# A hybrid state-space and attention layer on one core: the operand stacks of the next two heads begun at the first row block instead of the second, and the low parts of the first queries computed ahead of the other preparations

## The chip, the cores and the metric

The kernel runs on one core of a Trainium2 chip. The time is the device time of one execution in microseconds; the number that counts is the median over the runs. Engine names are those of the profile: PE (TensorE), DVE (VectorE), ACT (ScalarE), POOL (GpSimd) and SP (SyncE, which here only issues transfers). SPq, POOLq and so on are the engines' own queues of transfer issues.

## The reference, cut to what matters

One layer of an encoder runs over 512 prompt rows and 8 x 16 sample rows, 640 rows in all. Only branch B, the attention, is touched by the change: 8 heads of width 64, with a bias by relative position.

```python
z = rms_norm(x, p['g_mix']) @ p['w_in']
u, q, k, v, g_ssm, g_att = jnp.split(z, cuts, axis=-1)
# prompt, by chunks of 64 rows; a chunk reads itself and up to 8 chunks before it
sc = jnp.einsum('nihd,nkhd->nhik', qc, kb).astype(jnp.float32) * scale + bias
p = jax.nn.softmax(sc, axis=-1).astype(v.dtype)
return jnp.einsum('nhik,nkhd->nihd', p, vb)
# sample: 16 new rows of each of 8 streams read 512 cached rows and themselves
```

The other branch is a state-space scan (`s5`). Both branches are gated, added, projected, and followed by a convolutional feed-forward part.

## The kernel before

All products are made in float32r with operands cut into a high and a low part. A weight unit is 128x1024; for each of its eight blocks PE does three pairs of matmuls of 320 columns (`mm3`, line 115, outputs `pb`). This stream of projections runs without pause: after the state input come v, k, q and 16 units of gates. Each segment of six matmuls is one `tick`. Beside it a generator, `side_work`, is advanced by a fixed share of a step per tick: first the scan (`s5`), then the attention (`attention`). So everything of the attention stands between segments of the projections in PE's stream, and every engine executes its instructions strictly in the order in which the program wrote them (the schedule is manual).

The attention takes two heads at a time (`hp` = 0 to 3, heads 2hp and 2hp+1). Each pair has 32 steps of the generator: four row blocks `t` of 128 prompt rows (two prompts per block, one per head, three steps apart), and a sample group after blocks 1 and 3. The dictionary `plan` holds what is done at each step; things of the same step run in the order in which `at` wrote them.

- `prompt`: step +0 two matmuls of scores into the single bank `sS` (queries `qs`, then their low parts `ql`, both against `ks`), the bias and row maximum on DVE (line 733, reading the bias `pb`), the exponential on ACT (line 693); step +4 the normalisation (lines 739 and 740); step +8 the transposes into the single bank `sT` (line 746) and their evacuation `eT` by ACT (line 687) or DVE (line 689) in turn. `prompt_pv` multiplies with v.
- `sample`: the same for 64 sample rows (lines 794 to 833), with cached keys `kc` and values `vc`, two transfers each, three buffers each, loaded by `load_kv` one step after the previous group's scores.
- `stacks(hp)`: makes the operands `ks` and `qs` of a pair of heads in four steps: the high parts of k on ACT (line 663), the low parts of k on DVE (line 668), then two transfers on SP that put the low parts into the other half of the partitions of `ks` together with the high parts of q on ACT (line 663), then two transfers on SP that copy the halves of `qs` (line 672). Both tiles have two buffers.
- `q_low(hp)`: the low parts `ql` of the queries, two DVE instructions (line 703), one buffer.
- The preparations ahead of the first pair: POOL zeroes the idle halves of `ql` (line 698) and all of `QB` (line 848), SP loads two biases, keys and values, DVE copies the sample queries into `QB` (line 852, two copies for each pair of heads).

The names `pb` and `h` are used for more than one thing: `pb` is a bank of a projection on PE's lines and the bias in line 733; `h` is any 128x640 tile of the heap. `wr`, `wh`, `wl` are a weight unit, its high and its low part.

Of the kernel before, what the change touches and what calls it, by code (L numbers as in the profile page):

```python
# [43 lines left out]
def body(nc, tc, d, ctx):  # L44
# [12 lines left out]
    def nm(s):  # L57
        uid[0] += 1
        return f"{s}{uid[0]}"
# [585 lines left out]
    def half(h2):  # L645
        return slice(64 * h2, 64 * h2 + 64)
# [3 lines left out]
    def stacks(hp):  # L650

        if hp > 3:
            return []
        k, q = (qk[0].tile([128, 2, 512], F32R, tag=t, name=nm(t), bufs=2) for t in ("ks", "qs"))
        kl = ht(F32R, 512).rearrange("p (a b) -> p a b", a=1)
        st_[hp] = (k, q)

        def hi(dst, src):  # L660
            for h2 in range(2):
                s = half(h2)
                A.activation(dst[s, h2, :], src[s, 0:512], AF.Copy)

        def lo(dst, src, h):
            for h2 in range(2):
                s = half(h2)
                V.tensor_tensor(dst[s, 0, :], src[s, 0:512], h[s, h2, :].bitcast(F32), op=OP.subtract)

        def move(dst, src):  # L670
            for h2 in range(2):
                S.dma_start(dst[half(1 - h2), h2, :].bitcast(F32), src(h2).bitcast(F32))
        return [lambda: hi(k, kT[hp]), lambda: lo(kl, kT[hp], k),
                lambda: (move(k, lambda h2: kl[half(h2), 0, :]), hi(q, qT[hp])),
                lambda: move(q, lambda h2: q[half(h2), h2, :])]

    def attention():
# [22 lines left out]
        def q_low(hp):  # L700
            for h2 in range(2):
                s = half(h2)
                V.tensor_tensor(ql[s, h2, :], qT[hp][s, 0:512], st_[hp][1][s, h2, :].bitcast(F32), op=OP.subtract)
# [6 lines left out]
        def at(t, fn):  # L710
            plan.setdefault(t, []).append(fn)
# [3 lines left out]
        def load_pb(h):  # L715
            if h < 8:
                pbs[h] = ap_.tile([128, 512], F32, tag="pb", name=nm("pb"))
                S.dma_start(pbs[h], d["pbias"][h])

        def prompt(t0, h, t):  # L720
            hp, h2 = h // 2, h % 2
            w = 128 * (t + 1)
            m = {}

            def a():
                sc = smps("sS")
                k, q = st_[hp]
                n = max(w, 256)
                ts = slice(128 * t, 128 * t + 128)
                mm(sc[:, :n], q[:, h2, ts], k[:, h2, 0:n], True, False)  # L730
                mm(sc[:, :n], ql[:, h2, ts], k[:, h2, 0:n], False, True)
                sb, mx = tiles()
                V.tensor_tensor_reduce(sb[:, :w], sc[:, :w], pbs[h][:, 512 - w:512], 1.0, -3.0e38,
                                       op0=OP.add, op1=OP.max, accum_out=mx[:, 1:2])
                m["e"], m["mx"] = exps(sb, w, mx), mx

            def n():
                e, mx = m["e"], m["mx"]
                V.reciprocal(mx[:, 4:5], mx[:, 3:4])
                V.tensor_scalar(e[:, :w], e[:, :w], mx[:, 4:5], None, op0=OP.mult)  # L740

            def b():
                e = m["e"]
                pt = smps("sT")
                for k in range(t + 1):
                    PE.transpose(pt[:, k * 128:k * 128 + 128], e[:, k * 128:k * 128 + 128], ident)  # L746
                m["eT"] = ap_.tile([128, 512], F32, tag="eT", name=nm("eT"), bufs=3)
                evac(m["eT"][:, :w], pt[:, :w])

            at(t0, a)  # L750
            at(t0 + 4, n)
            at(t0 + 8, b)
            return m

        def prompt_pv(t0, hp, t, ms):

            def c():
                if t == 0:
                    po[0] = smps("sP")
                for k in range(t + 1):  # L760
                    for h2, m in enumerate(ms):
                        h = 2 * hp + h2
                        mm(po[0][half(h2), 128 * t:128 * t + 128], vt_[k][:, h * 64:h * 64 + 64],
                           m["eT"][:, k * 128:k * 128 + 128], k == 0, k == t)
                if t == 3:
                    evac(att[hp][:, 0:512], po[0])

            at(t0, c)

        def load_kv(hp, g4):  # L770
            if g4 == 0:
                sbs[hp] = ap_.tile([128, 576], F32, tag="sbias", name=nm("sbias"), bufs=1)
                S.dma_start(sbs[hp], d["sbias"][hp])
            kc, vc = [], []
            for i in range(2):
                k = ap_.tile([128, 2, 512], F32, tag="kc", name=nm("kc"), bufs=3)
                S.dma_start(k, d["kc"][hp, g4, :, 2 * i:2 * i + 2])
                kc.append(k)
            for i in range(2):
                v = ap_.tile([128, 2, 4, 128], F32, tag="vc", name=nm("vc"), bufs=3)  # L780
                S.dma_start(v, d["vc"][hp, g4, :, 2 * i:2 * i + 2])
                vc.append(v)
            kvs[hp, g4] = (kc, vc)

        def sample(t0, hp, g4):
# [55 lines left out]
            at(t0 + 12, c)  # L841
            at(t0 + 15, e_)

        load_pb(0)
        load_pb(1)
        load_kv(0, 0)
# [2 lines left out]
        for hp in range(4):  # L849
            for h2 in range(2):  # L850
                s = slice(64 * h2, 64 * h2 + 64)
                V.tensor_copy(QB[s, hp, :, h2, :], qT[hp][s, 512:640].rearrange("p (n i) -> p n i", n=8))
            if hp == 0:
                q_low(0)
            yield

        t0 = 0
        nxt = [None]
        for hp in range(4):
            for t in range(4):  # L860
                ms = []
                for h2 in range(2):
                    ms.append(prompt(t0, 2 * hp + h2, t))
                    if t == 3:
                        at(t0 + 1, lambda h=2 * hp + h2: load_pb(h + 2))
                    t0 += 3
                    if t == 1 and h2 == 1:
                        at(t0, lambda hp=hp: nxt.__setitem__(0, stacks(hp + 1)))
                        for j in range(4):
                            at(t0 + (1, 3, 5, 7)[j], lambda j=j: nxt[0] and nxt[0][j]())  # L870
                prompt_pv(t0 - 3 + 12, hp, t, ms)
                if t == 3 and hp < 3:
                    at(t0, lambda hp=hp: q_low(hp + 1))
                if t % 2:
                    i = 2 * hp + t // 2
                    sample(t0, hp, t // 2)
                    if i < 7:
                        at(t0 + 1, lambda i=i: load_kv((i + 1) // 2, (i + 1) % 2))
                    t0 += 4
# [29 lines left out]
    def side_work():  # L909
        qk[0] = qctx.enter_context(tc.tile_pool(name="qk", bufs=1))  # L910
        yield from s5()
        side[2] = 172 / (247 - clock[0])
        yield from attention()
        qctx.close()
# [223 lines left out]
    h2 = xctx2.enter_context(tc.tile_pool(name="heap2", bufs=1))  # L1138
# [599 lines left out]
```

## Time and profile before

| | |
|---|---|
| median of 3 runs | 943.2 us (942.18 to 1254.34) |
| the profiled execution | 940.75 us |
| its span | 938.9 us, so 1.85 us lie around the span |
| PE busy | 906.8 us (97% of the span) |
| DVE, ACT, POOL busy | 627.1, 441.5, 134.4 us |
| granted clock of PE, mean | 0.993 of full speed |
| stretch of the attention | about 182 to 323 us |

PE is the engine that sets the time, so what matters is where PE stands idle and where its clock falls. The profile puts each idle time down to what ended it.

### The profile page before, as it was taken

The numbers are of one execution on the slowest core, as the hardware profiler recorded it, in microseconds if no ns is written. First come the engines' busy times: TensorE is split into PE (matmuls) and PEld (weight loads), VectorE is DVE, ScalarE is ACT, GpSimd is POOL, SyncE is SP. The second block draws the span as 40 slices with busy tenths as digits, with TensorE's granted clock in tenths as the row PEclk, the third lists the DMA queues.
The fourth block names the chain that finished last, engine by engine and source line by source line (L and its number), as shares of the span: only waits on it lengthen the run. The fifth ranks groups of instructions, "written<-read, shape, count | busy, mean of one in ns | idle before, by whom it ended". The sixth has DMA issues, their size and how long they took to land.

```text
span 938.9 us, 16523 instructions
## 1 busy us (share of the span) xinstructions
PE 906.8 (97%) x6534; PEld 868.9 (93%) x6534; DVE 627.1 (67%) x1261; ACT 441.5 (47%) x689; POOL 134.4 (14%) x230
## 2 busy tenths in 40 slices
PE   8999999999899999999998999999999999999995
PEld 8978999987787899999998989999999999999994
DVE  6783996376675444586777887667666667667545
ACT  7244112353443464434676456554555545554531
POOL 0121402300000000000013122221122212222200
PEclk9999999999999999999999999999999999999998
DMA  6744428657566432243548689898788887888733
GB/s 227 206 134 127 132 71 92 214 192 256 170 183 235 111 104 68 69 127 132 140 105 190 147 164 226 181 201 188 180 197 191 192 201 179 186 200 194 180 60 112
DMA packets 62429, 151.76 MB, mean 162 GB/s; under 512 B 20945, under 2 KB 24209, under 8 KB 62353
## 3 DMA queue, kind: packets, MB, share of 16 engines
q1 hardware_dynamic: 45392, 95.90, 33.4%
q0 software_dynamic: 16096, 54.03, 30.4%
q8 instruction: 51, 0.84, 0.3%
q10 hardware_dynamic: 864, 0.78, 0.2%
q14 instruction: 26, 0.20, 0.1%
HBM read 114.56 MB, written 8.21 MB: 131 GB/s over the span
## 4 chain that ended last, share of the span: by engine, by line
PE 72%; DMA 9%; DVE 7%; ACT 5%; issue 4%; POOL 1%; SPq 1%; DVEq 0%; POOLq 0%; ACTq 0%
PE pb L115 40%; PE sS L115 9%; PE sT L115 7%; PE sX L115 7%; PE sP L115 5%; DMA wl<-in_w 3%; DMA o_s<-SV 2%; DMA qs<-qs 1%; DMA fl<-s 1%; DMA pb<-in_pbias 1%; PE sX L822 1%; DVE h L1536 1%; DMA wr<-in_w 1%; ACT wh L107 1%; PE sT L746 1%
## 5 line engine op out<-in xcount | busy, mean ns | idle before, releaser
L115 PE MATMUL pb<-h,wh 128*128 128x320 f32 (+2 forms) x2000 | 384.4, 313 | 4.7 <-DVE h L1517 1.2
L115 PEld LDWEIGHTS pb<-h,wh 128*128 128x128 f32 x2000 | 313.4, 189 | 10.5 <-issue 3.3
L115 PE MATMUL pb<-h,wl 128*128 128x320 f32 (+2 forms) x1000 | 230.3, 310 | 0.4 <-DVE wl L112 0.4
L115 PEld LDWEIGHTS pb<-h,wl 128*128 128x128 f32 x1000 | 167.9, 188 | 0.9 <-DVE wl L112 0.7
L1300 POOL DMA_DIRECT2D fl<-s x41 | 35.7, 871 | 440.7 <-PE pb L115 259.0
L107 ACT ACTIVATE wh<-wr 128x1024 fp32r<-128x1024 f32 x50 | 52.7, 1054 | 80.3 <-PE pb L115 59.9
L112 DVE TENSOR_TENSOR wl<-wr,wh 128x1024 fp32r<-128x1024 f32 x50 | 61.0, 1221 | 39.5 <-ACT wh L107 39.3
L115 PE MATMUL sS<-h,wh 128*128 128x320 f32 x336 | 74.7, 309 | 0.0
L115 PE MATMUL sX<-h,fh 128*128 128x320 f32 x320 | 71.6, 311 | 0.0
L1298 ACT ACTIVATE fl<-s 128x1024 fp32r<-128x1024 f32 x41 | 43.3, 1057 | 56.1 <-PE sT L115 48.7
L115 PEld LDWEIGHTS sS<-h,wh 128*128 128x128 f32 x336 | 56.2, 188 | 0.0
L115 PE MATMUL sS<-h,wl 128*128 128x320 f32 x168 | 52.2, 311 | 2.9 <-DMA wl<-in_w 2.9
L693 ACT ACTIVATE sb<-sb,mx 128x128 f32<-128x128 f32 (+4 forms) x40 | 24.2, 605 | 64.0 <-DVE mx L692 49.4
L115 PEld LDWEIGHTS sX<-h,fh 128*128 128x128 f32 x320 | 54.1, 190 | 0.0
L1300 POOL DMA_DIRECT2D wl<-in_w x43 | 38.1, 887 | 86.9 <-ACT wl L1298 79.6
L1371 ACT ACTIVATE tmp<-tmp 128x512 f32<-128x512 f32 x22 | 13.9, 633 | 76.0 <-DVE tmp L1368 76.0
L115 PE MATMUL sX<-h,fl 128*128 128x320 f32 x160 | 49.6, 310 | 0.0
L1298 ACT ACTIVATE wl<-wr 128x1024 fp32r<-128x1024 f32 (+1 forms) x43 | 43.5, 1011 | 7.1 <-PE sS L115 6.0
L115 PE MATMUL sT<-h,gh 128*128 128x320 f32 x176 | 40.1, 315 | 4.4 <-DVE u L1457 4.4
L1299 ACT ACTIVATE wh<-wr 128x1024 fp32r<-128x1024 f32 (+1 forms) x43 | 43.1, 1003 | 0.0
L1299 ACT ACTIVATE fh<-s 128x1024 fp32r<-128x1024 f32 x41 | 42.9, 1046 | 0.0
L1368 DVE SCALAR_TENSOR_TENSOR tmp<-tmp,vec 128x656 f32<-128x656 f32 x44 | 39.5, 897 | 0.7
(339 smaller groups left out, 1678.0 us busy)
## 6 DMA issues: line engine op xcount, KB each, us to landing
wr<-in_w SPq DMA_DIRECT2D x112, 512.0 KB, 4.6
fl<-s POOLq DMA_DIRECT2D x41, 512.0 KB, 5.8
wl<-in_w POOLq DMA_DIRECT2D x39, 512.0 KB, 8.3
kc<-in_kc SPq DMA_DIRECT2D x16, 512.0 KB, 6.6
vc<-in_vc SPq DMA_DIRECT2D x16, 512.0 KB, 5.7
x<-in_x SPq DMA_DIRECT2D x7, 320.0 KB, 5.9
pb<-in_pbias SPq DMA_DIRECT2D x8, 256.0 KB, 6.6
h<-in_x SPq DMA_DIRECT2D x6, 320.0 KB, 4.5
```

The lines of the kernel that those rows point to most:

```text
L107: A.activation(hi, raws[u], AF.Copy)
L112: V.tensor_tensor(lo, raws[u], hi.bitcast(F32), op=OP.subtract)
L115: PE.matmul(ps, lhs, rhs, start=start, stop=stop)
L693: A.activation(sb[:, :w], sb[:, :w], AF.Exp, bias=mx[:, 2:3], accum_out=mx[:, 3:4])
L746: PE.transpose(pt[:, k * 128:k * 128 + 128], e[:, k * 128:k * 128 + 128], ident)
L822: PE.matmul(sx[32 * n:32 * n + 32, 192:320], m["eT"][:, k * 128 + 32 * n:k * 128 + 32 * n + 32], vc[n // 2][:, n % 2, k, :], start=(k == 0 ...
L1298: A.activation(lo, src, AF.Copy, scale=-1.0)
L1299: A.activation(hi, src, AF.Copy)
L1300: G.dma_start(lo, src if again is None else again, accum_op=OP.add)
L1368: V.scalar_tensor_tensor(c_t, a_t[:, j:L + j], vcol(C_CW + 3 * f + j), c_t, op0=OP.mult, op1=OP.add)
L1371: A.activation(g_t[:, 0:512], c_t[:, 0:512], AF.Gelu_apprx_tanh)
L1536: V.scalar_tensor_tensor(o[:, 0:b - a], h_[i][:, a:b], vcol(C_GO + i), rs, op0=OP.mult, op1=OP.mult)
```

## The change

Three things are moved; no instruction is added or taken away. First, `q_low(0)` stands ahead of the first loads and of `QB`, not behind the first two copies into it. Second, the four steps of `stacks(hp + 1)` begin after the second prompt of row block 0, not of row block 1: they stand at steps +7, +10, +13 and +16 of a pair of heads where they stood at +13, +15, +17 and +19. Third, with that the first of them sit among the prompts of blocks 0 and 1.

```diff
+        q_low(0)
         load_pb(0)
         load_pb(1)
         load_kv(0, 0)
...
                 V.tensor_copy(QB[s, hp, :, h2, :], qT[hp][s, 512:640].rearrange("p (n i) -> p n i", n=8))
-            if hp == 0:
-                q_low(0)
             yield
...
                     t0 += 3
-                    if t == 1 and h2 == 1:
+                    if t == 0 and h2 == 1:
                         at(t0, lambda hp=hp: nxt.__setitem__(0, stacks(hp + 1)))
                         for j in range(4):
-                            at(t0 + (1, 3, 5, 7)[j], lambda j=j: nxt[0] and nxt[0][j]())
+                            at(t0 + (1, 4, 7, 10)[j], lambda j=j: nxt[0] and nxt[0][j]())
```

On DVE, at the start of the attention, this stands in the kernel before (`ql` is the low part of the queries, `QB` the sample queries, `sb` the scores of the first two prompts):

```order
L112 TENSOR_TENSOR wl_1972<-wr_1789,wh_1971 128x1024
L852 COPY QB<-h_1405 64x8x16 x2
L703 TENSOR_TENSOR ql<-h_1405,qs_1727 64x512 x2
L852 COPY QB<-h_1482 64x8x16 x2
L852 COPY QB<-h_1547 64x8x16 x2
L852 COPY QB<-h_1612 64x8x16 x2
L733 ISA sb_2100,mx_2101<-sS_2097,pb_2053 128x128
```

In the changed kernel, the same place on DVE:

```order
L703 TENSOR_TENSOR ql<-h_1405,qs_1727 64x512 x2
L853 COPY QB<-h_1405 64x8x16 x2
L853 COPY QB<-h_1482 64x8x16 x2
L853 COPY QB<-h_1547 64x8x16 x2
L853 COPY QB<-h_1612 64x8x16 x2
L733 ISA sb_2100,mx_2101<-sS_2097,pb_2055 128x128
```

The low parts moved past the first two copies; all eight copies still stand ahead of the first line 733.

On SP, in the second pair of heads (`hp` = 1), from the second sample group's loads to the next biases, before:

```order
L100 DMA wr_2470<-in_w 128x1024
L777 DMA kc_2615<-in_kc 128x1024
L777 DMA kc_2617<-in_kc 128x1024
L781 DMA vc_2619<-in_vc 128x1024
L781 DMA vc_2621<-in_vc 128x1024
L100 DMA wr_2656<-in_w 128x1024
L672 DMA ks_2589<-h_2591 64x512 x2
L672 DMA qs_2590<-qs_2590 64x512 x2
L718 DMA pb_2726<-in_pbias 128x512
L718 DMA pb_2778<-in_pbias 128x512
```

and in the changed kernel:

```order
L100 DMA wr_2470<-in_w 128x1024
L672 DMA ks_2518<-h_2520 64x512 x2
L777 DMA kc_2621<-in_kc 128x1024
L777 DMA kc_2623<-in_kc 128x1024
L781 DMA vc_2625<-in_vc 128x1024
L781 DMA vc_2627<-in_vc 128x1024
L672 DMA qs_2519<-qs_2519 64x512 x2
L100 DMA wr_2662<-in_w 128x1024
L718 DMA pb_2726<-in_pbias 128x512
L718 DMA pb_2778<-in_pbias 128x512
```

The transfers of `ks` moved ahead of the four loads of keys and values; those of `qs` moved ahead of one weight load only and still stand behind the last `vc`. The other two pairs show the same.

On DVE, in the same pair of heads, around the first sample group (lines 799 and 801 are its bias and maximum; `sX` is its second bank), before:

```order
L740 TENSOR_SCALAR sb_2521<-sb_2521,mx_2522 128x256
L689 COPY h_1405<-sX_2397 64x64
L799 ISA sb_2599,mx_2600<-sS_2592,sbias_2411 128x512
L799 ISA mx_2600 128x1
L801 ISA sb_2599,mx_2600<-sX_2593,sbias_2411,mx_2600 128x64
L801 ISA mx_2600 128x1
L692 TENSOR_SCALAR mx_2600<-mx_2600 128x1
L739 RECIPROCAL mx_2570<-mx_2570 128x1
L740 TENSOR_SCALAR sb_2569<-sb_2569,mx_2570 128x256
L689 COPY eT_2626<-sT_2623 128x256
L668 TENSOR_TENSOR h_2591<-h_1266,ks_2589 64x512 x2
L733 ISA sb_2642,mx_2643<-sS_2639,pb_2325 128x384
```

and in the changed kernel:

```order
L668 TENSOR_TENSOR h_2520<-h_1266,ks_2518 64x512 x2
L739 RECIPROCAL mx_2525<-mx_2525 128x1
L740 TENSOR_SCALAR sb_2524<-sb_2524,mx_2525 128x256
L689 COPY h_1405<-sX_2397 64x64
L799 ISA sb_2603,mx_2604<-sS_2596,sbias_2411 128x512
L799 ISA mx_2604 128x1
L801 ISA sb_2603,mx_2604<-sX_2597,sbias_2411,mx_2604 128x64
L801 ISA mx_2604 128x1
L692 TENSOR_SCALAR mx_2604<-mx_2604 128x1
L739 RECIPROCAL mx_2575<-mx_2575 128x1
L740 TENSOR_SCALAR sb_2574<-sb_2574,mx_2575 128x256
L689 COPY eT_2632<-sT_2629 128x256
```

The low parts of k (line 668) moved from just ahead of a prompt of block 2 to just ahead of the normalisation that stands before the sample group.

## Rows read from the trace of the kernel before

**Rows 1.** Waits of PE from 140 to 325 us: total, times, longest.

```profile
PE sS L115 <- DMA qs<-qs: 3.3, 3, 1.6
PE sT L810 <- ACT eT L687: 2.2, 2, 1.4
```

**Rows 2.** PE in order of time, first prompts: start, length, instruction, idle before.

```profile
186.94 0.36 PE L115 MATMUL sS<-ks,ql 128*128 128x256 f32 x1 [0.99 <-issue]
...
189.35 0.58 PE L115 MATMUL sS<-ks,qs 128*128 128x256 f32 x1 [1.18 <-DVE mx L733]
...
192.96 0.28 PE L115 MATMUL sS<-ks,qs 128*128 128x256 f32 x1
```

**Rows 3.** DVE in order of time, the same place.

```profile
185.68 0.46 DVE L852 COPY QB<-h 64x128 f32<-64x128 f32 x2 [8.62 <-POOL QB L848]
186.15 1.40 DVE L703 TENSOR_TENSOR ql<-h,qs 64x512 fp32r<-64x512 f32 x2
187.57 1.40 DVE L852 COPY QB<-h 64x128 f32<-64x128 f32 x6
189.00 0.29 DVE L733 CUSTOM_DVE_ANT_0 sb<-sS,pb 128x128 f32<-128x128 f32 x1
```

**Rows 4.** POOL in order of time, the same place.

```profile
183.66 1.10 POOL L698 MEMSET ql<- 64x512 f32 x2
184.70 0.94 POOL L848 MEMSET QB<- 128x1024 f32 x1
```

**Rows 5.** SP in order of time, the first load into the attention's pool.

```profile
182.34 0.80 SPq L718 DMA_DIRECT2D pb<-in_pbias  x2
```

**Rows 6.** By stretch: length; busy PE, PEld, DVE, ACT, POOL; clock, DMA share, GB/s.

```profile
188.00:189.00 1.00, 0.17 (x2) 0.00 (x0) 0.92 (x6) 0.00 (x0) 0.00 (x0) 1.00 1.03 377
...
191.00:192.00 1.00, 1.00 (x5) 1.00 (x5) 0.21 (x1) 1.00 (x5) 0.00 (x0) 0.50 1.03 422
...
250.00:260.00 10.00, 9.05 (x103) 8.09 (x104) 5.43 (x20) 2.58 (x9) 0.00 (x0) 1.00 0.65 224
```

**Rows 7.** PE in order of time, the other waits.

```profile
235.56 0.65 PE L810 MATMUL sT<-ident,sb 128*128 128x128 f32 x4 [1.42 <-ACT eT L687]
...
250.95 0.36 PE L115 MATMUL sS<-ks,qs 128*128 128x256 f32 x1 [1.65 <-DMA qs<-qs]
...
252.58 0.31 PE L115 MATMUL sS<-ks,qs 128*128 128x256 f32 x1
...
283.28 0.35 PE L115 MATMUL sS<-ks,qs 128*128 128x256 f32 x1 [1.41 <-DMA qs<-qs]
...
287.23 0.66 PE L810 MATMUL sT<-ident,sb 128*128 128x128 f32 x4 [0.76 <-ACT eT L687]
```

**Rows 8.** SP in order of time, ahead of the third pair of heads.

```profile
228.90 12.66 SPq L781 DMA_DIRECT2D vc<-in_vc  x2
...
242.09 1.11 SPq L672 DMA_DIRECT2D ks<-h  x2
243.28 1.19 SPq L672 DMA_DIRECT2D qs<-qs  x2
244.57 1.12 SPq L718 DMA_DIRECT2D pb<-in_pbias  x2
```

**Rows 9.** The tile qs: issue to landing over its eight transfers.

```profile
DMA to landing us min/median/max: 4.4/6.7/7.7
```

**Rows 10.** The tile pb, as a bias: issue to landing over its eight transfers.

```profile
DMA to landing us min/median/max: 2.7/6.6/8.4
```

**Rows 11.** DVE in order of time, first line 733 of the third and fourth pair.

```profile
252.15 0.29 DVE L733 CUSTOM_DVE_ANT_0 sb<-sS,pb 128x128 f32<-128x128 f32 x1 [1.98 <-DMA pb<-in_pbias]
...
285.62 0.29 DVE L733 CUSTOM_DVE_ANT_0 sb<-sS,pb 128x128 f32<-128x128 f32 x1 [3.64 <-DMA pb<-in_pbias]
```

**Rows 12.** ACT in order of time, high parts of k in the second pair.

```profile
230.71 1.27 ACT L663 ACTIVATE ks<-h 64x512 fp32r<-64x512 f32 x2
```

**Rows 13.** DVE in order of time, low parts of k in the second pair.

```profile
231.36 1.40 DVE L668 TENSOR_TENSOR h<-h,ks 64x512 fp32r<-64x512 f32 x2 [0.66 <-ACT ks L663]
```

## The prediction

> **What bounds the kernel now.** The table of times gives PE 97% of the span, so the first view is that of PE's waits, cut to the stretch in which the attention runs beside the projections. It lists three waits for the transfer of `qs`, 3.3 us, and two for an evacuation `eT` by ACT, 2.2 us [rows 1]; two more, 0.99 us put down to "issue" and 1.18 us to DVE's row maximum, lie at the very first prompts [rows 2]. The reader is to see that these 7.7 us are all that an edit to the order of the attention can win in PE's idle time. PE in order of time then says where each wait lies. The two at the first prompts are 2.4 us apart. [...] Single waits of 1.42, 1.65, 1.41 and 0.76 us stand later [rows 7]; the rest of the 3.3 us, about 0.25, lies ahead of the second pair of heads.
>
> DVE and POOL tell what the first two waits hang on. DVE does nothing until POOL has zeroed `QB`, then copies, makes `ql`, copies again, and only then reaches the first line 733 at 189.00 [rows 3]; POOL ended at 185.64 [rows 4]. The "issue" wait is thus a wait for `ql`, whose part for the first head ended 0.7 us after 186.15, just before PE went on [rows 2, 3]. SP's order tells the `qs` waits: the transfers of `ks` and `qs` stand behind a load of `vc` that blocks SP for 12.66 us [rows 8], and `qs` lands 4.4 to 7.7 us after its issue [rows 9].
>
> **The change part by part.** *Low parts first.* The two instructions keep their 1.40 us [rows 3]. They need the memory of the scan's pool, as the first bias load does, and that load was issued at 182.34 [rows 5]; they wait for no POOL instruction, since POOL zeroes the other halves. So `ql` should be done near 183.8, well before PE asks at 186.94 - 0.99 = 185.95 [rows 2]: the wait of 0.99 goes. What is late next is line 733. Its eight `QB` copies still need POOL's end at 185.64 and 0.46 + 1.40 = 1.86 us [rows 3, 4], so it starts near 187.55, and PE's second prompt 0.35 us later as before (189.00 to 189.35), near 187.9. PE would be there at 189.35 - 1.18 - 0.99 = 187.18 [rows 2], so a wait of about 0.7 stays. Gain 189.35 - 187.9 = 1.45 us. Bounds: 0 if `ql` waits for something that holds DVE till 185.6, 2.17 if both waits go.
>
> *The clock.* From the second to the third prompt PE takes 192.96 - 189.35 = 3.6 us at half clock [rows 2, 6], so 1.8 us are lost. The single wait of 1.65 us that ends at 250.95 [rows 7] is followed by no such fall: the clock from 250 to 260 us is 1.00 [rows 6]. With one wait of 0.7 us left I take the whole 1.8; bounds 0 and 1.8. [...]
>
> *The stacks six to three steps earlier.* Per pair they are two instructions on ACT for k and two for q, 1.27 us each two [rows 12], two on DVE, 1.40 us [rows 13], and four transfers on SP. No work is added.
>
> On SP the transfers of `ks` pass four loads of keys and values; those of `qs` pass one weight load and remain behind `vc`. At the third pair `vc` frees SP at 241.56, so `qs` is issued from about 241.65 instead of 243.28, its second half 0.6 us later near 242.25, with no `ks` and no weight between it and `vc` [rows 8]. With the median 6.7 us it lands at 248.95, with the longest 7.7 at 249.95 [rows 9]; PE asks at 250.95 - 1.65 = 249.30 [rows 7]. I take the median, because two 128 KB transfers and a weight have left its way: all three `qs` waits go, 3.3 us [rows 1]. The lower bound leaves 0.6 at each of the two long ones, 2.1 us. What is late next is the bias `pb`: the first line 733 of the pair waited for it until 252.15, and in the fourth pair until 285.62 [rows 11]. Its issue moves up by the 1.11 us of `ks` [rows 8], to 243.4, and by its median of 6.6 us it lands at 250.0 [rows 10]. PE wants the bank of the scores back 252.58 - 250.95 = 1.63 us after the pair's first score [rows 7], that is at 250.93, so line 733 must start by 250.5: covered by half a microsecond, and open by 1.2 us with the longest 8.4.
>
> In the fourth pair the same chain (bias, line 733, exponential, `eT`, line 810) gave the wait of 0.76 [rows 7]. PE comes 1.41 us earlier, the chain at least 1.1 by the issue alone, and more by the shorter way: I take 0.76 as gained, bounds 0 and 0.76.
>
> On ACT and DVE the old place crowded the wait of 1.42 us at 235.56 [rows 7]: 1.40 us of low parts stood ahead of a line 733 [rows 13]. They now stand before the sample group's line 799, whose exponential the same evacuation also stands behind on ACT. So the chain is relieved at its end and loaded at its start: I take half of the 1.40, gain 0.7, bounds 0 and 1.42.
>
> Against it, in the first pair the high parts of k now enter ACT while it catches up: from 191 to 192 us it is busy throughout [rows 6]. Behind that, 1.27 us [rows 12] make the next `eT` late for PE; of this I take a third, 0.4 us, since two segments of projections stand between the two uses of its bank; bounds 0 and 1.27. In the third pair ACT was busy for 2.58 and DVE for 5.43 of the 10 us from 250 [rows 6], so there, and in the second, whose blocks are the same, I count nothing. SP now waits for the low parts of k ahead of four loads; who waits is the sample group of step +28, some 15 steps away.
>
> Sum: 1.45 + 1.8 + 3.3 + 0.76 + 0.7 - 0.4 = 7.6 us. Against the profiled execution: span 938.9 - 7.6 = 931.3, with 1.85 around it 933.15. That execution lies 2.45 us under the median of 943.2, so the median becomes **935.6 us**. Behind the attention the loads and splits of weights are started by PE's own progress, so I see nothing that gives the time back.
>
> **The rivals.** *The clock falls all the same.* For it: a wait of 0.7 us and a slow start of the softmax chain remain at the same place. Against: two waits, 2.17 us, came ahead of the fall [rows 2]. Gain 7.6 - 1.8 = 5.8, time 937.4.
>
> *One wait takes the place of the other.* The transfers are late not for their place in the queue but for the way itself: `qs` is still behind `vc`, and `pb` behind `qs`. If PE stands as long at the two long transitions and at line 810, the gain is 1.45 + 1.8 + 0.25 + 0.7 - 0.4 = 3.8, time 939.4. For it speaks that `pb` landed 1.2 us after `qs` [rows 7, 11]; against, that two of the four slow transfers between partitions leave that stretch.
>
> *Slower.* The moved stacks sit in the wrong place: 1.27 us on ACT and 1.40 on DVE [rows 12, 13] stand ahead of prompts of blocks 0 and 1, which have the shortest matmuls to hide behind. It decides when ACT and DVE together have less than 2.67 us to spare between the prompts of steps +6 and +12. Fully exposed in three pairs this costs 8.0 us, and as the chain is then late the two `eT` waits stay: 1.45 + 1.8 + 3.3 - 8.0 = -1.45, time 944.65. Against it: from 250 to 260 us ACT was idle for 7.4 and DVE for 4.6 us [rows 6].
>
> *It doesn't do what it says.* `ql` is held till POOL is done and SP's order hides the earlier transfers: 0 to 1 us, 942.7.
>
> **How the numbers follow.** Forecast 935.6 with 0.6, the clock 0.13, the replaced wait 0.15, slower 0.05, nothing 0.07. The forecast's own bounds: all upper ends, 2.17 + 1.8 + 3.3 + 0.76 + 1.42 = 9.45, give 933.75; the lower ends of single terms are the rivals. The range reaches from 932.5 (a microsecond under that for the spread of the runs, whose lower two differ by 1.0) to 941.5, which takes in the replaced wait with 2 us above it and leaves out the last two cases. A difference of 2%, 18.9 us, is about what a measurement of this kernel can tell from no change; all cases lie far inside: faster by more 0.01, within 0.98, slower by more 0.01.
>
> **What would show it.** In the changed kernel's trace: `ql` at 182 to 184 us on DVE, ahead of POOL's end; no wait of PE at its first `ql` matmul, one of 0.5 to 1 us at the second prompt; clock 1.00 from 189 to 193; no PE wait for `qs`; line 733 of a pair waiting less than 1 us for `pb`; 0.5 to 1 us left near line 810 of the second pair. The prediction is wrong if the clock still falls at the start, or if new waits of PE for `eT` or for line 799 come up between steps +8 and +20 of a pair.

## The result, and the profile after

| | before | after |
|---|---|---|
| median of 6 runs each | 942.31 us | 934.2 us (933.25 to 935.76) |
| ratio of the times, 95% interval | | 0.9932 (0.9915 to 0.9949) |
| profiled execution, its span | 940.75, 938.9 us | 934.26, 932.4 us |
| mean granted clock of PE | 0.993 | 0.995 |

One run of before, at 1254.34 us, is left out of the ratio. The changed kernel is faster: the interval of the ratio stands for a gain of 4.8 to 8.0 us on 942.31 us. The two medians are 8.1 us apart, a little more than that. The forecast was 935.6 us, with a gain of 7.6 us.

The waits of PE from 140 to 325 us, in the changed kernel (total, times, longest), answer to [rows 1]:

```profile
PE sS L115 <- DVE mx L733: 1.0, 1, 1.0
PE sX L115 <- ACT h L687: 0.9, 1, 0.9
PE sX L115 <- DVE h L689: 0.8, 1, 0.8
PE sT L810 <- ACT eT L687: 0.5, 1, 0.5
PE sT L746 <- ACT eT L687: 0.2, 1, 0.2
```

No wait for `qs` is left, and the one put down to "issue" at the start is gone. What stays is 3.4 us where 7.7 stood. But three lines are new: PE waits twice for the evacuation of the bank `sX`, 1.7 us together, where the prediction had nothing, and 0.2 us for an `eT` at line 746, in the first pair.

At the first prompts, PE, DVE and POOL of the changed kernel in order of time, against [rows 2 to 4]:

```profile
186.40 0.28 PE L115 MATMUL sS<-ks,qs 128*128 128x256 f32 x1
...
188.66 0.39 PE L115 MATMUL sS<-ks,qs 128*128 128x256 f32 x1 [0.99 <-DVE mx L733]
...
190.77 0.28 PE L115 MATMUL sS<-ks,qs 128*128 128x256 f32 x1
```

```profile
183.09 1.40 DVE L703 TENSOR_TENSOR ql<-h,qs 64x512 fp32r<-64x512 f32 x2 [4.71 <-DMA qs<-qs]
186.41 1.87 DVE L853 COPY QB<-h 64x128 f32<-64x128 f32 x8 [1.91 <-POOL QB L849]
188.31 0.29 DVE L733 CUSTOM_DVE_ANT_0 sb<-sS,pb 128x128 f32<-128x128 f32 x1
```

```profile
185.43 0.95 POOL L849 MEMSET QB<- 128x1024 f32 x1
```

`ql` is done before POOL is, and the eight copies run in one go of 1.87 us from POOL's end to the first line 733. The execution runs about 0.7 us later than the profiled one of before at this place (the last matmul of the scan ends at 183.00, in before at 182.28), so times are compared from that matmul's end below. The stretches answer to [rows 6]; the last figures but two are the granted clock:

```profile
188.00:189.00 1.00, 0.34 (x2) 0.34 (x3) 0.72 (x5) 0.14 (x1) 0.00 (x0) 1.00 0.90 322
191.00:192.00 1.00, 1.00 (x10) 1.00 (x8) 0.91 (x6) 1.00 (x3) 0.00 (x0) 1.00 0.98 332
250.00:260.00 10.00, 9.11 (x104) 7.08 (x103) 6.68 (x25) 3.45 (x9) 0.00 (x0) 1.00 0.57 190
```

From 191 to 192 us the clock is 1.00 and ten matmuls ran, where five ran at 0.50.

SP ahead of the third pair, against [rows 8]:

```profile
225.41 1.19 SPq L672 DMA_DIRECT2D ks<-h  x2
...
227.76 11.43 SPq L781 DMA_DIRECT2D vc<-in_vc  x2
239.28 1.10 SPq L672 DMA_DIRECT2D qs<-qs  x2
...
241.10 0.93 SPq L718 DMA_DIRECT2D pb<-in_pbias  x2
```

`qs` still stands behind the loads of `vc`, which hold SP for 11.43 us, but is the first thing behind them. The landing of the eight `qs` transfers and of the biases, from 170 to 330 us, against [rows 9, 10]:

```profile
DMA to landing us min/median/max: 4.6/5.3/6.8
```

```profile
DMA to landing us min/median/max: 2.7/5.9/8.0
```

And PE at three waits of the sample groups. The one of 1.42 us at line 810 in [rows 7] is now 0.47; the two of `sX` are new:

```profile
227.00 0.43 PE L115 MATMUL sX<-h,QB 128*128 128x64 f32 x2 [0.77 <-DVE h L689]
...
233.18 0.65 PE L810 MATMUL sT<-ident,sb 128*128 128x128 f32 x4 [0.47 <-ACT eT L687]
...
259.08 0.43 PE L115 MATMUL sX<-h,QB 128*128 128x64 f32 x2 [0.89 <-ACT h L687]
```

What the first of them waits for is seen on DVE, ahead of it, in order of time:

```profile
224.63 0.15 DVE L692 TENSOR_SCALAR mx<-mx 128x1 f32<-128x1 f32 x1
224.70 1.40 DVE L668 TENSOR_TENSOR h<-h,ks 64x512 fp32r<-64x512 f32 x2
226.13 0.16 DVE L739 RECIPROCAL mx<-mx 128x1 f32<-128x1 f32 x1
226.33 0.35 DVE L740 TENSOR_SCALAR sb<-sb,mx 128x256 f32<-128x256 f32 x1
226.71 0.23 DVE L689 COPY h<-sX 64x64 f32<-64x64 f32 x1
226.97 0.69 DVE L799 CUSTOM_DVE_ANT_0 sb<-sS,sbias 128x512 f32<-128x512 f32 x1
```

The low parts of k, 1.40 us, stand ahead of the copy out of `sX` that frees the bank for the sample group's second score product; between them are only the two short instructions of a normalisation. PE asks for the bank at 227.00 - 0.77 = 226.23 us, the copy ends at 226.94, and PE starts at 227.00.

The wait in the third pair is put down to ACT, but the chain is the same. The bank is emptied by two copies, one of them on ACT, and ACT's waits for DVE's. DVE first, then ACT:

```profile
256.68 1.39 DVE L668 TENSOR_TENSOR h<-h,ks 64x512 fp32r<-64x512 f32 x2
...
258.57 0.21 DVE L689 COPY h<-sX 64x64 f32<-64x64 f32 x1
```

```profile
258.81 0.22 ACT L687 ACTIVATE h<-sX 64x64 f32<-64x64 f32 x1 [1.42 <-DVE h L689]
```

Three more executions were profiled, two of before and one of after, both kernels unchanged. The score matmul of each of the 32 prompts and the last matmul of line 833 are the same points of the program in every kernel, and their distance from the end of the last scan matmul repeats closely at first: 7.07, 7.07 and 7.07 us to the second prompt in before, 5.66 and 5.66 in after. Up to the end of the second pair it repeats within 0.15 us, at the end of the attention within 0.7 us in before and 0.3 us in after. The whole attention, to the start of its last matmul of line 833, took 141.99, 142.70 and 142.60 us before, 134.84 and 135.12 after: means 142.43 and 134.98, a gain of 7.45 us against the sum of 7.6.

### The profile page after: what moved, and what is told of

Its sections match the earlier page's. It is cut to its first block, busy times and chain, and to the rows that moved or that the text cites. A ratio compares the mean times of both kernels' runs of the same rounds, so it can differ in the third digit from the quotient of the medians.

```text
span 932.4 us, 16524 instructions
## 1 busy us (share of the span) xinstructions
PE 903.9 (97%) x6534; PEld 867.4 (93%) x6534; DVE 627.6 (67%) x1261; ACT 441.5 (47%) x689; POOL 135.1 (14%) x230
## 4 chain that ended last, share of the span: by engine, by line
PE 73%; DVE 10%; ACT 6%; DMA 5%; issue 4%; POOL 1%; SPq 0%; DVEq 0%; POOLq 0%; ACTq 0%
PE pb L115 40%; PE sS L115 9%; PE sT L115 8%; PE sX L115 7%; PE sP L115 5%; DMA wl<-in_w 3%; DMA o_s<-SV 2%; PE sT L746 1%; PE sX L822 1%; DVE h L1535 1%; ACT wh L107 1%; PE sS L794 1%; DVE wl L112 1%; DVE h L1209 1%; DVE sm L271 1%
```

## The experiments

The times of the medians are blurred by some 2 us: PE's mean granted clock differs from execution to execution of one kernel (0.984 to 0.997 in 23 of before, last section). So each kernel is also read by two figures of its profiled execution: the length of the attention, counted as above, with the gain over the 141.99 us of before, and the gain at single prompts. The 141.99 us are the shortest of before's three lengths (mean 142.43), so a total gain may be read 0.4 us too low, and totals that differ by less than 0.7 us aren't told apart by them; steps within one execution are sharper.

| kernel | median us | ratio to before, 95% | attention us | gain us |
|---|---|---|---|---|
| only the low parts of q moved | 939.66 | 0.9983 (0.9962 to 1.0004) | 137.97 | 4.02 |
| only the stacks moved | 936.19 | 0.9952 (0.9933 to 0.9971) | 138.17 | 3.82 |
| changed, low parts of k behind the sample group | 931.85 | 0.9906 (0.9879 to 0.9934) | 132.77 | 9.22 |
| changed, copies to `QB` spread over steps 1 to 5 | 932.7 | 0.9925 (0.9898 to 0.9952) | 134.53 | 7.46 |
| changed, six copies made twice | 936.13 | 0.9962 (0.9943 to 0.9981) | 137.93 | 4.06 |
| changed, transfers of the stacks late | 939.19 | 0.9997 (0.9976 to 1.0017) | 140.54 | 1.45 |
| both mends: low parts of k, copies far out | 932.1 | 0.9915 (0.9889 to 0.9942) | 132.10 | 9.89 |

Gain at the score matmul of a prompt over the profiled before, us (pair of heads, then the prompt in it; the kernels in the order of the table, the changed kernel first):

| prompt | changed | low parts only | stacks only | k behind | copies spread | copies twice | transfers late | both mends |
|---|---|---|---|---|---|---|---|---|
| 1, second | 1.41 | 1.41 | 0.00 | 1.42 | 2.56 | -0.12 | 1.41 | 2.56 |
| 1, third | 2.91 | 2.92 | -0.02 | 2.93 | 4.17 | 0.05 | 2.92 | 4.17 |
| 1, fifth | 2.84 | 2.90 | -0.08 | 2.85 | 3.12 | -0.21 | 2.84 | 4.10 |
| 1, sixth | 2.38 | 2.90 | -0.53 | 2.84 | 2.67 | -0.66 | 2.40 | 4.10 |
| 2, fourth | 2.98 | 2.96 | 0.05 | 3.44 | 3.26 | -0.06 | 2.90 | 4.42 |
| 2, fifth | 2.15 | 2.96 | -0.78 | 3.44 | 2.43 | -0.90 | 2.07 | 4.43 |
| 2, seventh | 3.10 | 2.95 | 0.18 | 4.19 | 3.38 | 0.05 | 3.02 | 5.17 |
| 3, first | 4.90 | 3.04 | 1.98 | 6.00 | 5.17 | 1.86 | 2.96 | 6.96 |
| 3, fourth | 5.00 | 3.02 | 2.07 | 6.09 | 5.27 | 1.95 | 2.96 | 7.06 |
| 3, fifth | 4.05 | 3.03 | 1.12 | 6.10 | 4.31 | 1.00 | 1.96 | 7.06 |
| 4, second | 6.08 | 3.10 | 2.87 | 8.13 | 6.36 | 3.03 | 0.38 | 8.94 |
| 4, third | 7.17 | 4.03 | 3.84 | 9.22 | 7.45 | 4.08 | 1.46 | 9.89 |

**Only the low parts of the queries moved.** Theory: the gain is the sum of two separate parts, the start and the stacks. The rival: one part makes the other worth less.

```diff
+        q_low(0)
         load_pb(0)
...
-            if hp == 0:
-                q_low(0)
```

> Only the low parts of the first queries are moved; the stacks stay at steps +13 to +19. Theory: the change is two parts that add up, and this one is worth what the first three prompts show in the two traces, 1.4 us of waits and 1.5 us of half clock: 2.9 us under the kernel before, the first wait for ql gone, one wait near 1 us at the second prompt, the clock at 1.00, and the three waits for qs (3.3 us) as before. [...] Rival (the parts are not independent, because the first pair's moved stacks need the time won at the start): 1 us or less.

The start gives 1.41 us at the second prompt and 2.92 at the third, as in the changed kernel, with a clock of 1.00 from 187 to 194 us. The three waits for `qs` (3.3 us) and the 1.4 us at line 810 of the second pair stand as before. At the third prompt of the fourth pair another 0.93 us come that no moved instruction explains; more on that below. With them the attention gains 4.02 us where 2.9 were expected. The interval of this kernel's ratio reaches 1.0004, so its median alone shows no gain.

**Only the stacks moved.** The same edit the other way round, on the changed kernel: `q_low(0)` behind the first two copies.

> Only the stacks are moved; the low parts of the first queries stay behind the first two copies. Theory: 4.2 us under the kernel before (the rest of the 7.1 us won in the stretch), with the two waits of 0.99 and 1.18 us and the half clock at the first prompts as before, no wait for qs, and the two new waits for the bank sX of 0.8 to 0.9 us. [...] Rival (not independent): the first pair has more room here, since PE runs at half clock there, so that the waits of the sample group differ and the gain is over 5 us or under 3.

Its waits of PE from 140 to 325 us:

```profile
PE sS L115 <- DVE mx L733: 1.2, 1, 1.2
PE sS L115 <- issue: 1.0, 1, 1.0
PE sX L115 <- ACT h L687: 0.9, 1, 0.9
PE sX L115 <- DVE h L689: 0.8, 1, 0.8
PE sT L810 <- ACT eT L687: 0.5, 1, 0.5
PE sT L746 <- ACT eT L687: 0.2, 1, 0.2
```

Both first waits are back, the clock falls to 0.50 with them (191 to 194 us), and no wait for `qs` is there. So the `qs` waits go by the stacks alone. Also by the stacks alone come the two waits for `sX` and the 0.45 us lost in the first pair. The start's 2.92 us and this kernel's 3.82 make 6.74; both at once gain 7.16. The parts add, within 0.4 us. (The gains of the whole attention, 4.02 and 3.82, make 7.84: the microsecond in the fourth pair stands in both.)

**The low parts of k behind the sample group.** Theory: the two `sX` waits come from the 1.40 us of line 668 ahead of the copy that frees the bank. The rival: they come from the earlier start of everything, or from the high parts on ACT.

```diff
-  at(t0 + (1, 4, 7, 10)[j], lambda j=j: nxt[0] and nxt[0][j]())
+  at(t0 + (1, 7, 7, 10)[j], lambda j=j: nxt[0] and nxt[0][j]())
```

> The changed kernel with the low parts of k at step +13 instead of +10, behind the sample group's maximum on DVE and not ahead of the evacuation of the sample group before it; the transfers of ks stay ahead of the loads. Theory: the two waits for sX (0.77 and 0.89 us) come from these 1.40 us of DVE ahead of the evacuation that frees the bank, so they go, and the wait before line 810 grows by up to 0.7 in the second pair: 1.0 to 1.7 us under the changed kernel. Rival (the sX waits come from the high parts of k on ACT): they stay and the time is that of the changed kernel within 0.5 us.

DVE of this kernel at the same place, in order of time:

```profile
223.66 0.16 DVE L692 TENSOR_SCALAR mx<-mx 128x1 f32<-128x1 f32 x1
223.73 0.15 DVE L739 RECIPROCAL mx<-mx 128x1 f32<-128x1 f32 x1
223.92 0.35 DVE L740 TENSOR_SCALAR sb<-sb,mx 128x256 f32<-128x256 f32 x1
224.65 0.23 DVE L689 COPY h<-sX 64x64 f32<-64x64 f32 x1 [0.38 <-ACT h L687]
225.34 0.69 DVE L799 CUSTOM_DVE_ANT_0 sb<-sS,sbias 128x512 f32<-128x512 f32 x1 [0.47 <-PE sS L794]
...
226.59 1.40 DVE L668 TENSOR_TENSOR h<-h,ks 64x512 fp32r<-64x512 f32 x2
```

The same 1.40 us now run behind the sample's maximum, and DVE waits for PE at line 799. Both `sX` waits are gone, and the gain over the changed kernel is 9.22 - 7.16 = 2.06 us: 0.83 in the second pair and 0.95 in the third, 0.46 in the first, less some 0.2 at line 810 (wait 0.7 instead of 0.5); 1.0 to 1.7 were expected. So the loss in the first pair was line 668 too: the high parts of k on ACT, which the prediction charged with it, stood where they were.

**The copies to `QB` spread out.** Theory: what is left of the first wait is the copies' 1.87 us ahead of line 733.

```diff
-        for hp in range(4):
+        def qb_copy(hp):
...
+        for hp in range(4):
+            at((1, 2, 4, 5)[hp], lambda hp=hp: qb_copy(hp))
```

> The changed kernel with the eight copies into QB moved behind the first prompts (steps +1, +2, +4, +5); they are read at step +12. Theory: the wait of 0.99 us at the second prompt hangs on the copies, which stand ahead of the first line 733 and wait for POOL; it goes, 0.8 to 1.0 us under the changed kernel. Rival (the first line 733 waits for the bias transfer or for the table load's chain): 0.3 us or less.

The wait at the second prompt is gone (gain 2.56 instead of 1.41). But the same copies then stand in the chain of the next prompts, PE waits 0.5 us for line 733 at the fourth, and by the fifth only 0.28 us of the 1.15 are left. At the end of the attention it is 0.30 us, where 0.8 to 1.0 were expected: the wait hung on the copies, as the theory said, but most of the gain didn't last.

**Six of the copies made twice.** The same data are copied once more, which adds 1.40 us to DVE's work ahead of the first line 733. Theory: a longer wait makes the clock fall there. The rival: the fall has nothing to do with the wait's length.

```diff
+            if hp:
+                for h2 in range(2):
+                    s = slice(64 * h2, 64 * h2 + 64)
+                    V.tensor_copy(QB[s, hp, :, h2, :], qT[hp][s, 512:640].rearrange("p (n i) -> p n i", n=8))
```

> The changed kernel with six of the eight copies into QB done twice, 1.40 us more of DVE ahead of the first line 733 and nothing else: the single wait at the second prompt grows from 0.99 to 2.4 us, about what the two waits of the kernel before made together. Theory (the fall of the clock comes from the idle time of PE that comes together at this place): the clock falls to 0.50 as in the kernel before, and the stretch of the attention is 1.4 us longer for the wait and 1.5 us for the clock, 2.9 us over the changed kernel. [...]

PE at the second prompt, and the stretches around it:

```profile
190.11 0.39 PE L115 MATMUL sS<-ks,qs 128*128 128x256 f32 x1 [2.52 <-DVE mx L733]
```

```profile
190.00:191.00 1.00, 0.89 (x5) 0.89 (x6) 0.52 (x6) 0.69 (x1) 0.00 (x0) 0.78 1.03 422
191.00:192.00 1.00, 1.00 (x6) 1.00 (x5) 0.14 (x1) 0.99 (x3) 0.00 (x0) 0.50 1.01 414
```

Of the two waits of before this kernel makes one, and the clock falls all the same, so it doesn't take two. The wait grew by 1.53 us and the clock fell to 0.50; at the third prompt the kernel is 2.86 us behind the changed one, 1.53 of them by the wait and 1.33 by the clock. Behind that its steps are those of the changed kernel within 0.25 us.

**The transfers of the stacks late, their arithmetic early.** Theory: the `qs` waits hang on the place of the transfers on SP alone. The rival: on the earlier high and low parts.

```diff
-            at(t0 + (1, 4, 7, 10)[j], lambda j=j: nxt[0] and nxt[0][j]())
+        for j in range(5):
+            at(t0 + (1, 4, 7, 11, 13)[j], lambda j=j: nxt[0] and nxt[0][j]())
```

(`stacks` returns five steps for the later pairs: high k, low k, high q, move k, move q.)

> The changed kernel with the high and low parts of k and the high parts of q where the change put them (+7, +10, +13), and the four transfers of a pair at steps +17 and +19, both behind the last load of vc, as in the kernel before. Theory (the qs waits go because ks is out of the queue ahead of qs and the bias): the three waits for qs come back, 3.3 us over the changed kernel in the stretch, while the two sX waits (1.7 us) and the shorter wait before line 810 of the second pair (0.5 us) stay as in the changed kernel. Rival (they go because the parts are ready earlier): the qs waits stay away and the time is that of the changed kernel.

PE at the start of the third and the fourth pair, and the clock behind the second wait:

```profile
247.89 0.36 PE L115 MATMUL sS<-ks,qs 128*128 128x256 f32 x1 [1.69 <-DMA qs<-qs]
...
281.43 0.36 PE L115 MATMUL sS<-ks,qs 128*128 128x256 f32 x1 [1.81 <-DMA qs<-qs]
```

```profile
282.00:284.00 2.00, 2.00 (x11) 1.96 (x10) 0.01 (x1) 0.00 (x0) 0.00 (x0) 0.51 1.05 408
```

The two long waits are back, with the losses of the early low parts still there (-0.44, -0.83, -1.00), and behind the second the clock fell, which cost another 1.37 us. The third wait, 0.28 us ahead of the second pair, didn't come back, so for that one the place of the transfers isn't shown to be the cause. The attention is 7.16 - 1.45 = 5.71 us longer than in the changed kernel, where 3.3 were expected. This kernel keeps the start's 2.9 us, and what follows is a loss; its median is that of before (ratio 0.9997).

**Both mends together.** The low parts of k as above, and the copies to `QB` at steps 1, 17, 23 and 30. The cut shows the line of the copies against the kernel with the copies spread.

```diff
-            at((1, 2, 4, 5)[hp], lambda hp=hp: qb_copy(hp))
+            at((1, 17, 23, 30)[hp], lambda hp=hp: qb_copy(hp))
```

> The changed kernel with the low parts of k at step +13 and the copies into QB spread over the first pair of heads, two each at steps +1, +17, +23 and +30, so that only two stand near the first prompts. Theory: what the two mends showed adds up: 2.07 us less in the stretch of the attention than the changed kernel for the low parts, and the whole of the first wait, 1.15 us, since the crowding of DVE that gave most of it back with all eight copies at steps +1 to +5 does not come: 3.1 us under the changed kernel in the stretch, about 931 us. Rival (DVE has no room there either): 2.1 us and the same time as with the first mend alone.

Its only wait of PE from 140 to 325 us:

```profile
PE sT L810 <- ACT eT L687: 0.7, 1, 0.7
```

The attention is 2.74 us shorter than in the changed kernel, where 3.1 were expected, and 9.89 shorter than before. Of the 1.15 us of the copies 0.67 are left at its end; no wait shows where the rest went. The median, 932.1, is that of the kernel with the first mend alone (931.85): the 0.67 us are lost in the spread. Both medians lie under the changed kernel's 934.2, but they were taken at another time and the intervals of the ratios overlap; that the mends help is shown by the `sX` waits that are gone and by the steps at the prompts.

**Both kernels unchanged, in further executions.**

> The kernel before, unchanged, in another execution. If the two waits of 0.99 and 1.18 us at the first prompts make TensorE's clock fall, the granted clock reads 0.50 in some microsecond between 189 and 194 again, and the third prompt's score matmul starts about 1.5 us later than in the changed kernel, counted from the end of the last scan matmul. If the fall depends on the moment at which the waits come, it is absent in some of the executions, and then the third prompt starts only about 1.4 us (the low parts' share) later than in the changed kernel, instead of 2.9 us. The waits for the queries of the later pairs and the ones at line 810 are there in either case, and the attention takes 140 to 143 us from the end of the last scan matmul to the last matmul of line 833.

> The kernel before once more, with the same expectation as the execution ahead of it: a fall to 0.50 between 189 and 194 us if the waits alone decide, none in some executions if the moment decides as well.

> The changed kernel, unchanged, in another execution. Granted clock 1.00 in each microsecond from 187 to 193 if a wait of 1.0 us is too short to make it fall there, 0.50 in one of them if the moment decides. The two waits of 0.9 and 0.8 us for the bank of the fixed stacks' products are there again at the second and the third pair, since the order of the instructions makes them. The wait of 2.9 us near 503 us is followed by a fall to 0.50 or by none, whichever the moment gives. Attention 134 to 136 us.

One time each: 942.93 and 943.34 us for before, 935.09 for after. In both of before the clock falls to 0.50 from 190 to 193 us, and the third prompt stands 10.72 and 10.68 us behind the scan's end (10.68 in the first execution). In after it stands at 7.77 in both, at clock 1.00. All waits recur at their places; those for `qs` total 3.8 and 3.7 us in before, where 3.3 were read, and before has one more, of 0.2 to 0.3 us for line 733 in the fourth pair.

## Why the prediction was right

The main mechanisms held: the first wait, the clock at the start and the two long waits for `qs` went for the reasons given. That the number came so near is in part luck. Two losses of together 1.78 us were left out of the sum, and three terms happened to bring 1.5 us more than their forecast, while the others brought 0.4 less. The median came out 1.4 us under the forecast although the attention gained a little less than the sum; that is inside the scatter of the runs. The measured terms sum to 6.94 us; what is left to the 7.16 are steps of 0.1 us or less.

| term | forecast | measured | shown by |
|---|---|---|---|
| low parts of q first | 1.45 | 1.41 | low parts only |
| clock at the start | 1.8 | 1.50 | low parts only, copies twice |
| waits for `qs` | 3.3 | about 4.2 | stacks only; the two long ones also transfers late |
| line 810, second pair | 0.7 | 0.96 | stacks only |
| line 810, fourth pair | 0.76 | 1.09 | cause open: comes without the moved stacks too |
| first pair | -0.4 | -0.46 | k behind |
| second and third pair | 0 | -0.83, -0.95 | k behind |

The measured values are differences between rows of the prompt table, or between such prompts of the changed kernel. The `qs` term is 0.42 + 0.08 at the first two prompts of the second pair, 1.80 + 0.08 of the third and 1.57 + 0.27 of the fourth.

*Low parts first.* The step held: line 733 stands 188.31 - 183.00 = 5.31 us behind the scan's end, forecast 187.55 - 182.28 = 5.27. PE came 0.23 us earlier than forecast, so the wait left is 0.99, not 0.7.

*The clock.* The forecast halved the 3.6 us between the prompts; they became 2.11 in the changed kernel, so 1.50 us were lost and not 1.8. Part of that is that the clock was back before the third prompt (its mean from 192 to 193 us is 0.66); the rest stays open. The rival that the clock falls all the same had a chance of 0.13. At this place it is refuted as far as twelve executions go: the clock fell in all five with waits of 2.17 us in two parts or 2.5 in one (before three times, stacks only, copies twice), and in none of the seven with at most 1.0 us.

*The transfers.* `qs` was forecast at 241.65 us on SP. In the changed kernel it is issued at 239.28; with the 3.1 us gained up to there added and the 0.72 of the later scan taken off, that is 241.66. It also landed in a median of 5.3 us, not 6.7. The kernel with late transfers shows for the two long waits that the place on SP does it. The term was too small because it was read off the profile's idle times: between prompts a wait for `qs` costs more than its idle time, 1.80 us for the 1.65 and 1.57 for the 1.41, and in the kernel with late transfers 1.86 for 1.69 and 1.98 for 1.81; some 0.4 us more come at the second prompts of the three pairs. The rival that one wait takes the other's place fails with it: no DVE wait for a bias is longer than 1.0 us in either execution of the changed kernel.

*Second and third pair.* Here the prediction failed: "in the second, whose blocks are the same, I count nothing". The idle shares of 10 us stretches were taken as cover. Yet the 1.40 us stood, in the order of DVE, just ahead of a copy that helps to free a single bank, and PE asked for that bank 0.13 us after they had ended, before the copy had begun. The two waits of 0.77 and 0.89 us cost 0.83 and 0.95 us at the prompts behind them. The prediction moved line 668 "before the sample group's line 799", looked at line 799 and the exponential, and not at the copy between them. Moving line 668 by three steps took both waits away.

*The first pair.* The size was right, by luck, and the cause wrong: it was line 668 on DVE, not the high parts of k on ACT. The late `eT` that the prediction named is there, the 0.2 us at line 746. Line 668 delays the sample group's maximum, and with it the exponential on ACT, which starts 197.26 - 183.00 = 14.26 us behind the scan's end, and 13.79 in the kernel with line 668 moved; behind that ACT makes the high parts of q, and only then this `eT`:

```profile
198.04 1.27 ACT L663 ACTIVATE qs<-h 64x512 fp32r<-64x512 f32 x2
199.33 0.38 ACT L687 ACTIVATE eT<-sT 128x256 f32<-128x256 f32 x1
```

The prediction called itself wrong "if new waits of PE for `eT` or for line 799 come up between steps +8 and +20 of a pair". This one, at step +17, is such a wait, and the two for `sX` at step +12 lie in the same steps, for a bank that it didn't name. By its own sign this part of the prediction failed.

*Line 810 of the fourth pair.* About 1 us was gained in every kernel that came there earlier, also in the one with only the low parts of q moved (0.93), whose order there is that of before, and in none of the three executions of before. In before the first line 733 of the pair starts 8.5 to 9.0 us after the bias's issue on SP, waiting for it, in the low-parts kernel 7.5 (281.82 - 274.33). So the transfer landed earlier after its issue by a microsecond or more; what it shares its way with was not tried, and stays open. The prediction's reason, the earlier issue of the bias behind `ks`, isn't needed for this term.

## What to carry to other kernels

A busy share over ten microseconds says nothing about one slot: before an instruction is moved ahead on an engine that runs its instructions in the order written (as DVE did here, where the copy out of `sX` began at 226.71 us, behind the 1.40 us of line 668 moved ahead of it), list each instruction that it now precedes and ask which of them frees a single buffer, and when the next engine asks for that buffer. Early arithmetic and early transfers are two decisions: what the two long waits for transfers gave here came from the transfers' place in the queue, and what was lost came from one arithmetic step that could have stood three steps of the generator later. Where the median is blurred, distances between fixed points of the program in one execution tell more: here they repeated within 0.15 us over the first two pairs, and within 0.7 us at the end of the attention.

## What the runs showed of the hardware

A wait of the same 2.89 us was followed by a fall of the clock to 0.50 in one kernel and by a clock of 1.00 in another. Near 500 us every kernel has a wait of PE for `u`. In two kernels it ended at the same time. First the kernel with the low parts of k behind the sample group, PE and stretches:

```profile
500.13 0.57 PE L115 MATMUL sT<-h,gh 128*128 128x320 f32 x2 [2.89 <-DVE u L1456]
```

```profile
502.00:504.00 2.00, 2.00 (x16) 2.00 (x15) 1.69 (x4) 0.63 (x1) 1.03 (x4) 1.00 1.11 246
```

Then the one with both mends:

```profile
500.12 0.56 PE L115 MATMUL sT<-h,gh 128*128 128x320 f32 x2 [2.89 <-DVE u L1459]
```

```profile
502.00:504.00 2.00, 2.00 (x10) 2.00 (x9) 1.26 (x3) 0.63 (x1) 0.60 (x3) 0.50 1.11 250
```

Sixteen matmuls in one, ten in the other. Over all twelve profiled executions the wait is 2.89 us (3.11 in the first of before); eight show the fall behind it and four don't, and each kernel that ran more than once showed it each time. The two executions above are of two different programs, and no run shows what decides between a fall and none. At the first prompts the fall went with the length of the wait in twelve of twelve: it came behind waits of together 2.17 us and more, and not behind 1.0 us and less.

Nor does the longer wait always bring the fall. Behind the wait of 1.81 us in the kernel with late transfers the clock read 0.51 from 282 to 284 us. Behind this longer one, in the second execution of before, the next score matmul starts 253.37 - 251.74 = 1.63 us later, just as behind the wait of 1.65 us in the first execution (252.58 - 250.95), where the clock read 1.00 from 250 to 260 us:

```profile
251.74 0.36 PE L115 MATMUL sS<-ks,qs 128*128 128x256 f32 x1 [1.93 <-DMA qs<-qs]
...
253.37 0.28 PE L115 MATMUL sS<-ks,qs 128*128 128x256 f32 x1
```

The spread of the times goes with the granted clock: of 23 runs of before, taken beside those of the first four experiments, the fastest took 936.86 us at a mean clock of 0.997, the slowest 946.6 at 0.984. The kernel with both mends ran 932.61 us in its profiled execution at a mean clock of 0.993, the one with the first mend alone 929.67 at 0.997, though its attention is 0.67 us longer.
